# A gated hybrid encoder layer: background weight work in tiles of its own and partly behind the projections, and merge sums that stay on chip

## The chip, the cores and the metric

The kernel runs on one core of one Trainium2 chip. The metric is the device time of one execution in microseconds (us), lower is better. It is given as the median of several runs. A profile comes from one execution of its own. The engines are named as the profile names them: PE multiplies matrices (PEld is its weight load), DVE does elementwise work on vectors, ACT does copies, casts and activations, POOL and SP mainly issue transfers here.

## The reference

One layer of an encoder over 1024 tokens of width 1024, all in float32:

```
h = x + 1/2 * SwiGLU_1(RMSNorm(x))                       # FFN 1, inner width 2816
u = RMSNorm(h)
[qA|kA|vA|qB|kB|vB|gA|gB] = u @ W_in                     # one input projection, width 4352
yA = NeighbourhoodAttention2D(qA, kA, vA)                # 8 heads of 64, 8x16 window, bias table
yB = WindowedGQA(rope(qB), rope(kB), vB)                 # 8 query heads, 2 key heads, window 128, sink
h = h + (sigmoid(gA) * (yA @ W_A) + sigmoid(gB) * (yB @ W_B)) @ W_out      # the merge
h = h + 1/2 * SwiGLU_2(RMSNorm(h))                       # FFN 2, same size as FFN 1
y = RMSNorm_final(h)
SwiGLU(x) = (silu(x @ w_gate) * (x @ w_up)) @ w_down
```

## The kernel before, in words

**Numbers as pairs.** Every operand of a matmul is held as two parts of reduced float32, high and low. `split` writes them: ACT casts the high part, DVE subtracts it from the source to get the low part. One product is then three matmuls in `mm3` (high x high in line 149, high x low in 151, low x high in 153). A program line of a helper therefore stands for many places.

**Strassen products.** The large products are done in 2 x 2 blocks with seven block products, P1 to P7. In the FFNs and the projections, a "product" in the code is one of these for one slice of 128 columns: twelve matmuls 512 wide. `products` runs through them in a fixed order `seq`, prepares the weights of about eight products ahead (`prep_until`), multiplies, and after each product drains its results from PSUM and calls `at_end(n)`, where n counts the products that are still to come (FFN 1 has 154 products, n runs down to 0; the projections have 98).

**Stages in order.** FFN 1 (its first 30 products in an order written out by hand), its down projection (class `Down`), the input projections, the attention with the gates and the branch B product as filler, the branch A products, the merge with W_out (`Down` again, with the name `down`, later `merge`), FFN 2 and its down projection, the final norm.

**Background of FFN 1.** While FFN 1 multiplies, the kernel prepares weights that later stages read back ready split. `later(n, f, ...)` books a step, `behind_ffn1(n)` runs the steps booked for n. There are three sets:

- W_B and the gate columns of W_in that the projections leave out: 8 + 12 = 20 pieces. `wab_fetch` loads a piece into a tile tagged `hs` (six buffers of 128 x 512), `wab_split` writes its two parts into two more `hs` tiles, `wab_put` stores both with a transfer each from POOL's queue. The fetch is booked at n = 108 - 2i, the split two products later, the put one later.
- W_A: `wa_fetch`, `wa_split`, `wa_put`, sixteen splits. These use `split_out`, whose output tile comes from `halves_out`: two buffers tagged `xs`, and as every third one the tile tagged `gain`.
- W_out: `wo_fetch`, `wo_split`, `wo_put`. For each of four row blocks p there are seven splits, 28 in all, with block sums of the weight formed in place in the fetched `hs` tiles; `put_out` stores 512 KB a time into `wo_d`. They are booked from n = 44 down to n = 6.

The splits of these sets are held in program order on their engine by `pin`. Other instructions are ordered by a planner that works with costs when the program is built; it also hands the buffers of a tag to the next tile as they come free. The queue of an engine is then fixed: an instruction that waits holds up what stands behind it on the same engine. `hook(n, f, ...)` books steps behind the projections in the same way.

**Branch A and the gates.** For a row block p, `a_product(p, k)` makes product P1 to P7 in PSUM, `a_keep` lets ACT copy P1, P5 and P6 out, and `a_gate(p, k)` does the rest on DVE: line 1414 adds PSUM to the kept part, line 1416 multiplies by (1 + tanh of the gate) into the gate's own tile `ra`, and for k = P4 and P3, line 1418 adds the whole finished chunk `r` (128 x 1024) to `merged(dc)`, where branch B's part already stands. The gate chunks are fetched by `a_fetch(p)` into tiles tagged `raw` (four buffers, line 1468), and `a_open` applies the tanh on ACT (line 1473). So the buffer of one chunk is free for the fetch of a later one when line 1418 has read it. Branch A runs for p = 0, 1 and then for p = 2, 3, with `both`, `weights`, `a_gate` in the order of the diff's last part.

**Merge.** `Down` multiplies `merged` by the four row blocks of W_out: 7 products x 4 row blocks = 28 entries of twelve matmuls, in the order P2, P1, P5, P6, P3, P7, P4. An entry needs its left operand split (`prep`, lines 95 and 98) and its right operand from `wo_d` (line 591). P1, P2 and P4 take quarters of `merged`. The left operands of P5, P6, P3 and P7 are sums of quarters: `combine(p)` forms four of them on DVE (line 1691) and stores them to `left_d` in DRAM (line 1692); `load_left` brings them back into `raw` tiles (line 577). `combine(0)` and `combine(1)` stand between the branch A products P1/P5 and P2 of p = 2, 3, and `combine(2)` and `combine(3)` behind the first two prepared entries. `evict` (line 639) adds results from PSUM to the residual.

Of the kernel before, what the change touches and what calls it, by code (L numbers as in the profile page):

```python
# [31 lines left out]
def f32v(ap):  # L32
    return ap.bitcast(F32)
# [3 lines left out]
def trunk_kernel(ctx, tc, x, xt, n1, wg1, wu1, wd1, nm, win, rpb, sink, wa, wb, wout,  # L37
                 n2, wg2, wu2, wd2, nf, c_rope, c_mask_a, c_mask_b, out):
    nc = tc.nc
# [9 lines left out]
    ps = ctx.enter_context(tc.tile_pool(name="ps", bufs=4, space=bass.MemoryType.PSUM))  # L49
    dram = ctx.enter_context(tc.tile_pool(name="dram", bufs=1, space=bass.MemoryType.DRAM))  # L50
# [3 lines left out]
    def nm_(s):  # L54
        uid[0] += 1
        return f"{s}_{uid[0]}"
# [8 lines left out]
    ar = {}  # L65
# [26 lines left out]
    pin = tc.keep_in_program_order  # L92
# [15 lines left out]
    def w_cols(w, c0, n=P):  # L108
        return w[:, c0:c0 + n].rearrange("(c p) f -> p c f", p=P)
# [51 lines left out]
    def res(t):  # L161

        return fx[t] if t < 4 else fa[:, (t - 4) * 1024:(t - 3) * 1024]
# [538 lines left out]
    down = down_ffn(wd1[0], lambda t: x2[t])  # L702
# [46 lines left out]
    NG = len(groups)  # L749
    gates = [dc for dc in [*range(8, 16), *range(8)] if 18 + dc not in sum((p for g in groups for p in g), ())]  # L750
    wg_d = dram.tile([len(gates), 2, P, 1024], F32, name="wg_d")
    cast = {}

    def hs(dt):
        return main.tile([P, 512], dt, tag="hs", bufs=6, name=nm_("hs"))

    def wab_fetch(i):
        r = cast[i] = hs(F32)
# [5 lines left out]
        nc.sync.dma_start(r.rearrange("p (c f) -> p c f", f=P), src)  # L764

    def wab_split(i):
        r, h, l = cast[i], hs(F32R), hs(F32R)
        pin(nc.scalar.copy(h, r))
        pin(nc.vector.tensor_tensor(l, r, f32v(h), op=ALU.subtract))
        cast[i] = h, l  # L770

    def wab_put(i):
        g, half = divmod(i - NC8, 2)
        for k, a in enumerate(cast.pop(i)):
            dst = wb_d[i, :, k * 512:k * 512 + 512] if g < 0 else wg_d[g, k, :, half * 512:half * 512 + 512]
            nc.gpsimd.dma_start(dst, f32v(a))

    wo_d = dram.tile([len(PRODUCTS), 4, P, 1024], F32, name="wo_d")
    nout = [0]
    wo = {}  # L780

    def halves_out():

        nout[0] += 1
        if nout[0] % 3 == 0:
            return const.tile([P, 1152], F32R, tag="gain", bufs=1, name=nm_("made"))[:, :1024]
        return main.tile([P, 1024], F32R, tag="xs", bufs=2, name=nm_("made"))

    def split_out(key, src):

        n = src.shape[1]
        o = cast[key] = halves_out()[:, :2 * n]
        pin(nc.scalar.copy(o[:, :n], src))
        pin(nc.vector.tensor_tensor(o[:, n:], src, f32v(o[:, :n]), op=ALU.subtract))

    def put_out(key, dst):
        nc.gpsimd.dma_start(dst, f32v(cast.pop(key)))
# [17 lines left out]
    def later(n, *f):  # L815
        background.setdefault(int(n), []).append(f)
# [22 lines left out]
        put_out((g, p), wa_d[p, g, :, :512] if g == 3 else wa_d[p, g])  # L839

    for i in range(NC8 + 2 * len(gates)):
        for e, f in ((3, wab_put), (2, wab_split), (0, wab_fetch)):
            later(108 - 2 * i - e, f, i)
    for p in range(4):
        later(67 - 5 * p, wa_fetch, p)
        for g in range(4):
            later(64 - 5 * p - 5 * g // 4, wa_split, g, p)
            later(63 - 5 * p - 5 * g // 4, wa_put, g, p)
    step = [44 - 1.34 * k for k in range(29)]
    for p in range(4):  # L850
        later(step[7 * p] + 2, wo_fetch, p)
        for j, k in enumerate(("P2", "P1", "P3", "P5", "P7", "P6", "P4")):
            later(step[7 * p + j], wo_split, k, p)
            later(step[7 * p + j] - 1, wo_put, k, p)

    def behind_ffn1(n):
        down.at_end(n)
# [376 lines left out]
    def hook(n, *f):  # L1234
        hooks.setdefault(n, []).append(f)

    for c in range(5):
        n = 14 * (NG - 1) - 8 - 6 * c
        hook(n, rope_load, c)
        for step in range(3):  # L1240
            hook(n - 4 - step, rope, step, c)
# [166 lines left out]
    def a_gate(p, k):  # L1408

        key, add, dc, n = dict(P2=("X", "P1", p, L), P7=("W", "P5", p + 4, R), P4=("W", None, p + 4, L), P3=("Y", "P6", p, R))[k]  # L1410
        src, r = bk[key, p], mix["ra", dc]
        if add is not None:
            t = kept_a[p, add]
            nc.vector.tensor_tensor(t, src, t, op=ALU.add)
            src = t
        nc.vector.scalar_tensor_tensor(out=r[:, n], in0=r[:, n], scalar=1.0, in1=src, op0=ALU.add, op1=ALU.mult)
        if k in ("P4", "P3"):
            nc.vector.tensor_tensor(merged(dc), merged(dc), r, op=ALU.add)

    def merged(dc):  # L1420
        return slot((0, 1, 2, 3, 24, 25, 26, 27)[dc])
# [248 lines left out]
    def load_h(t):  # L1670
        nc.sync.dma_start(res(t), h_d[t * P:(t + 1) * P, :])


    left_d = dram.tile([4, 4, P, 512], F32, name="left_d")

    def quarter(k, p):
        m = merged(p + (4 if k in ("P2", "P4") else 0))
        return m[:, :512] if k in ("P1", "P2") else m[:, 512:]

    loads = {t: [lambda d, t=t: load_h(t)] for t in range(NTT)}  # L1680
    loads[0].append(lambda d: d.load_left(2))
    down = Down(4, None, 0.5, {}, quarter, {k: left_d[i] for i, k in enumerate(("P5", "P6", "P3", "P7"))},
                loads, (8, 10), late=True, right=wo_d)

    def combine(p):
        a11, a12, a22 = [quarter(k, p) for k in ("P1", "P2", "P4")]
        a21 = merged(p)[:, 512:]
        s = [res(4 + 2 * (p % 2) + k // 2)[:, k % 2 * 512:k % 2 * 512 + 512] for k in range(4)]
        for i, (a, b, op) in enumerate(((a21, a22, ALU.add), (s[0], a11, ALU.subtract), (a12, s[1], ALU.subtract),
                                        (a11, a21, ALU.subtract))):  # L1690
            nc.vector.tensor_tensor(s[i], a, b, op=op)
            nc.gpsimd.dma_start(left_d[i, p], s[i])

    def both(p, *ks):
        for k in ks:
            for q in (p, p + 1):
                a_product(q, k)
                if k in ("P1", "P5", "P6"):
                    a_keep(q, k)
# [7 lines left out]
    for p in (0, 2):  # L1707
        if p:
            both(p, "P1", "P5")
            a_open(3)  # L1710
            combine(0)
            both(p, "P2")
            combine(1)
        both(p, "P6")
        if p == 0:
            a_open(1)
            weights(2, 0)
        for q in (p, p + 1):
            a_gate(q, "P2")
        both(p, "P3")  # L1720
        if p == 0:
            weights(2, 1)
        both(p, "P7")
        if p == 0:
            weights(2, 2)
        for q in (p, p + 1):
            a_gate(q, "P3")
            a_gate(q, "P7")
        both(p, "P4")
        if p == 0:  # L1730
            weights(2, 3)
        for q in (p, p + 1):
            a_gate(q, "P4")
            if p == 0:
                a_fetch(q + 2)
        if p == 0:
            a_open(2)
            for t in range(4):
                new_fx(t)
            new_ar(2)  # L1740
    down.prep_until(2)
    for p in (2, 3):
        combine(p)


# [2 lines left out]
    down = down_ffn(wd2[0], lambda t: h_d[t * P:(t + 1) * P, :])  # L1748
# [22 lines left out]
    late = {}  # L1771
# [111 lines left out]
```

## Time and profile before

| | |
|---|---|
| median of 3 runs | 1930.12 us (1927.0 to 1930.21) |
| profiled execution: its time, its span | 1927.95 us, 1926.2 us |
| PE, PEld busy | 1905.3 us (99%), 1594.1 us (83%) |
| DVE, ACT, POOL busy | 1474.7 us (77%), 961.4 us (50%), 323.6 us (17%) |
| TensorE clock granted, mean | 0.998 |
| DMA | 374.24 MB, mean 194 GB/s |

The span runs from the first to the last instruction, and all times within it are counted from its start. A busy share is the part of the span in which an engine had at least one instruction running. Matmuls overlap on PE, so a matmul's duration is longer than the distance between two starts. A view by windows gives the busy time of each engine within a stretch. A timeline gives start and duration of instructions, with the idle time before them and what ended it in brackets; "x2" there are two merged into one row. "DMA to landing" is the time from the issue of a transfer to its completion.

### The profile page before, as it was taken

The numbers are of one execution on the slowest core, as the hardware profiler recorded it, in microseconds if no ns is written. First come the engines' busy times: TensorE is split into PE (matmuls) and PEld (weight loads), VectorE is DVE, ScalarE is ACT, GpSimd is POOL, SyncE is SP. The second block draws the span as 40 slices with busy tenths as digits, with TensorE's granted clock in tenths as the row PEclk, the third lists the DMA queues.
The fourth block names the chain that finished last, engine by engine and source line by source line (L and its number), as shares of the span: only waits on it lengthen the run. The fifth ranks groups of instructions, "written<-read, shape, count | busy, mean of one in ns | idle before, by whom it ended". The sixth has DMA issues, their size and how long they took to land.

```text
span 1926.2 us, 26199 instructions
## 1 busy us (share of the span) xinstructions
PE 1905.3 (99%) x9020; PEld 1594.1 (83%) x9020; DVE 1474.7 (77%) x2598; ACT 961.4 (50%) x1876; POOL 323.6 (17%) x505
## 2 busy tenths in 40 slices
PE   9999999999999999999999999999999999999998
PEld 7888788888788888898898887788888888888886
DVE  8988878868977778755887999689675566569864
ACT  7533444544346543444888985265333333344453
POOL 0013322213600112211111200010110001005211
PEclk9999999999999999999999999999999999999999
DMA  7258777799353368753647968963422323492341
GB/s 268 94 183 275 260 257 273 296 347 364 96 194 132 111 189 244 232 175 126 178 124 221 280 210 317 371 245 120 148 104 103 121 88 109 145 363 88 119 139 60
DMA packets 184325, 374.24 MB, mean 194 GB/s; under 512 B 18432, under 2 KB 80768, under 8 KB 184192
## 3 DMA queue, kind: packets, MB, share of 16 engines
q1 hardware_dynamic: 146064, 253.01, 39.6%
q0 software_dynamic: 37264, 118.51, 17.9%
q8 instruction: 71, 1.16, 0.2%
q10 hardware_dynamic: 864, 1.05, 0.2%
q14 instruction: 62, 0.51, 0.1%
HBM read 248.25 MB, written 126.02 MB: 194 GB/s over the span
## 4 chain that ended last, share of the span: by engine, by line
PE 85%; DVE 5%; issue 4%; DMA 4%; POOL 1%; ACT 0%; SPq 0%; POOLq 0%; DVEq 0%; ACTq 0%
PE g L149 16%; PE g L151 16%; PE g L153 16%; PE d L153 10%; PE d L151 10%; PE d L149 10%; PE d L1597 2%; DVE ws L98 1%; PE g L1616 1%; PE d L1576 1%; PE d L1577 1%; PE g L1611 1%; DVE ar L98 1%; DMA ar<-in_ffn_w_down_dram 1%; DMA raw<-hid 1%
## 5 line engine op out<-in xcount | busy, mean ns | idle before, releaser
L149 PE MATMUL g<-ar,ws 128*128 128x512 f32 x1072 | 410.3, 394 | 3.5 <-ACT fx L477 1.5
L151 PE MATMUL g<-ar,ws 128*128 128x512 f32 x1072 | 407.4, 390 | 0.0
L153 PE MATMUL g<-ar,ws 128*128 128x512 f32 x1072 | 406.0, 390 | 0.0
L151 PE MATMUL d<-ar,ws 128*128 128x512 f32 x712 | 277.3, 389 | 0.6 <-DVE ar L994 0.6
L149 PE MATMUL d<-ar,ws 128*128 128x512 f32 x712 | 277.6, 390 | 0.2 <-ACT ar L992 0.2
L153 PE MATMUL d<-ar,ws 128*128 128x512 f32 x712 | 277.2, 389 | 0.0
L153 PEld LDWEIGHTS g<-ar,ws 128*128 128x128 f32 x1072 | 201.1, 188 | 41.9
L151 PEld LDWEIGHTS g<-ar,ws 128*128 128x128 f32 x1072 | 201.0, 188 | 41.1 <-DVE ar L98 0.3
L149 PEld LDWEIGHTS g<-ar,ws 128*128 128x128 f32 x1072 | 198.2, 188 | 41.9 <-issue 2.6
L332 DVE TENSOR_TENSOR ws<-raw,ws 128x512 fp32r<-128x512 f32 x216 | 147.6, 688 | 80.5 <-ACT ws L325 79.9
L325 ACT CAST ws<-raw 128x512 fp32r<-128x512 f32 x216 | 132.6, 620 | 132.4 <-PE g L153 62.5
L151 PEld LDWEIGHTS d<-ar,ws 128*128 128x128 f32 x712 | 133.7, 188 | 28.9 <-DVE ar L994 1.2
L149 PEld LDWEIGHTS d<-ar,ws 128*128 128x128 f32 x712 | 133.6, 188 | 28.3 <-ACT ar L992 0.8
L153 PEld LDWEIGHTS d<-ar,ws 128*128 128x128 f32 x712 | 133.7, 188 | 27.9 <-DVE ws L332 0.4
L95 ACT CAST ws<-raw 128x512 fp32r<-128x512 f32 x98 | 61.1, 623 | 139.6 <-PE d L153 57.9
L444 POOL DMA_DIRECT2D hid<-fx x91 | 49.4, 543 | 330.1 <-DVE fx L504 209.2
L98 DVE TENSOR_TENSOR ws<-raw,ws 128x512 fp32r<-128x512 f32 x98 | 73.5, 752 | 39.4 <-ACT ws L95 39.4
L95 ACT CAST ar<-raw 128x512 fp32r<-128x512 f32 (+1 forms) x86 | 55.9, 653 | 94.2 <-PE g L151 52.9
L98 DVE TENSOR_TENSOR ws<-ar,ws 128x512 fp32r<-128x512 f32 x94 | 79.5, 848 | 16.1 <-ACT ws L95 16.0
L149 PE MATMUL g<-ws,ws 128*128 128x512 f32 x232 | 90.9, 392 | 0.0
L153 PE MATMUL g<-ws,ws 128*128 128x512 f32 x232 | 90.4, 390 | 0.0
L151 PE MATMUL g<-ws,ws 128*128 128x512 f32 x232 | 90.3, 389 | 0.0
(360 smaller groups left out, 3916.5 us busy)
## 6 DMA issues: line engine op xcount, KB each, us to landing
raw<-hid SPq DMA_DIRECT2D x70, 512.0 KB
hid<-fx POOLq DMA_DIRECT2D x91, 256.0 KB, 2.7
ar<-in_ffn_w_down_dram SPq DMA_DIRECT2D x32, 512.0 KB
raw<-in_ffn_w_up_dram SPq DMA_DIRECT2D x31, 512.0 KB
wo_d<-made POOLq DMA_DIRECT2D x28, 512.0 KB, 5.8
raw<-in_ffn_w_gate_dram SPq DMA_DIRECT2D x27, 512.0 KB
hid<-fa POOLq DMA_DIRECT2D x51, 256.0 KB, 2.7
ar<-zs_d POOLq DMA_DIRECT2D x48, 256.0 KB, 7.7
```

What stands on the lines that cost most here:

```text
L95: hi = nc.scalar.copy(dst_hi, src)
L98: (eng or nc.vector).tensor_tensor(dst_lo, src, f32v(dst_hi), op=ALU.subtract)
L149: nc.tensor.matmul(b, lhs[0], r[0], start=first, stop=False, **kw)
L151: nc.tensor.matmul(b, lhs[0], r[1], start=False, stop=False, **kw)
L153: nc.tensor.matmul(b, lhs[1], r[0], start=False, stop=last, **kw)
L325: nc.scalar.copy(w[0][:, :512], a)
L332: nc.vector.tensor_tensor(w[0][:, 512:], a, f32v(w[0][:, :512]), op=ALU.subtract)
L444: nc.gpsimd.dma_start(hid[PRODUCTS.index(p), i], src)
L1576: nc.tensor.matmul(b[:, :nw], un["q"][s], un["kd"][s][:, k0 * P:k1 * P], start=True, stop=False)
L1577: nc.tensor.matmul(b[:, :nw], un["q"][s], un["kl"][s][:, k0 * P:k1 * P], start=False, stop=True)
L1597: nc.tensor.transpose(pt[:, i * P:(i + 1) * P], un["pr"][s][:, i * P:(i + 1) * P], ident)
L1611: nc.tensor.matmul(o[:, s], un["v"][s][:, un["k0"] + i, :], un["p"][s][:, i], start=i == 0, stop=i == last)
```

## The change

It does four things.

1. The pieces of W_B and of the gates use `split_out` and `halves_out` for their split parts, so that `hs` holds only their raw form, and both parts go out with one transfer instead of two. The bookings become n = 95 - 1.6i for the split, five products earlier for the fetch, one later for the put. W_A is booked over n = 66 to 38.
2. W_out's row blocks 0 and 1 are booked behind FFN 1 from n = 36 at a step of 1.5 products, and row blocks 2 and 3 behind the projections from n = 27 at a step of 1.34. There `halves_out` gives only the two `xs` buffers (`kept_gain` is emptied).
3. `combine` no longer writes `left_d`. Its sums stay in two tile groups, `ar[1]` and `ar[4]`, taken anew as float32, and `prep` splits them from there. All four calls come after the first six entries of the merge are prepared.
4. Line 1418's addition stays on DVE only for P4 with p = 2 and 3. The other six chunks are added by a transfer from POOL's queue that accumulates `r` onto `merged(dc)`.

```
+    def wab_split(i):
+        split_out(i, wab_raw.pop(i))
...
+            put_out(i, wg_d[g].rearrange("k p f -> p k f")[:, :, half * 512:half * 512 + 512], 2)
...
     for i in range(NC8 + 2 * len(gates)):
-        for e, f in ((3, wab_put), (2, wab_split), (0, wab_fetch)):
-            later(108 - 2 * i - e, f, i)
+        n = int(95 - 1.6 * i)
+        for e, f in ((1, wab_put), (0, wab_split), (-5, wab_fetch)):
+            later(n - e, f, i)
     for p in range(4):
-        later(67 - 5 * p, wa_fetch, p)
...
+        later(66 - 6 * p, wa_fetch, p)
+        for g, e in enumerate((0, 1, 3, 4)):
+            later(61 - 6 * p - e, wa_split, g, p)
+            later(60 - 6 * p - e, wa_put, g, p)
+
+    def wo_steps(put, first, step, ps):
+        for m, p in enumerate(ps):
+            for j, k in enumerate(("P2", "P1", "P3", "P5", "P7", "P6", "P4")):
+                n = int(first - step * (7 * m + j))
+                if j == 0:
+                    put(n + 5 - m, wo_fetch, p)
+                put(n, wo_split, k, p)
+                put(n - 1, wo_put, k, p)
+
+    wo_steps(later, 36, 1.5, (0, 1))
...
+    kept_gain.clear()
+    wo_steps(hook, 27, 1.34, (2, 3))
...
-        if k in ("P4", "P3"):
+        if k == "P4" and p >= 2:
             nc.vector.tensor_tensor(merged(dc), merged(dc), r, op=ALU.add)
+        elif k in ("P4", "P3"):
+            nc.gpsimd.dma_start(merged(dc), r, accum_op=ALU.add)
...
+    COMBINED = ("P5", "P6", "P3", "P7")
     def quarter(k, p):
+        if k in COMBINED:
+            i = COMBINED.index(k)
+            return ar[(1, 4)[i // 2]][:, 2 * (i % 2) + p // 2, p % 2 * 512:p % 2 * 512 + 512]
...
-    loads[0].append(lambda d: d.load_left(2))
-    down = Down(4, None, 0.5, {}, quarter, {k: left_d[i] for i, k in enumerate(("P5", "P6", "P3", "P7"))},
-                loads, (8, 10), late=True, right=wo_d)
+    down = Down(4, None, 0.5, {}, quarter, {}, loads, (8, 10), late=True, right=wo_d)
...
-        s = [res(4 + 2 * (p % 2) + k // 2)[:, k % 2 * 512:k % 2 * 512 + 512] for k in range(4)]
+        s = [quarter(k, p) for k in COMBINED]
...
             nc.vector.tensor_tensor(s[i], a, b, op=op)
-            nc.gpsimd.dma_start(left_d[i, p], s[i])
...
             both(p, "P1", "P5")
             a_open(3)
-            combine(0)
             both(p, "P2")
-            combine(1)
         both(p, "P6")
...
-    down.prep_until(2)
-    for p in (2, 3):
+    down.prep_until(6)
+    for g in (1, 4):
+        new_ar(g, F32)
+    for p in range(4):
         combine(p)
```

More of the change, by code (lines that the diff above doesn't have):

```diff
@@ L751, in trunk_kernel @@
     wg_d = dram.tile([len(gates), 2, P, 1024], F32, name="wg_d")
-    cast = {}
+    cast, wab_raw = {}, {}
     def hs(dt):
@@ L757, in wab_fetch @@
     def wab_fetch(i):
-        r = cast[i] = hs(F32)
+        r = wab_raw[i] = hs(F32)
         if i >= NC8:
@@ L764, in wab_fetch @@
         nc.sync.dma_start(r.rearrange("p (c f) -> p c f", f=P), src)
[L766 to L776, printed above, removed]
     wo_d = dram.tile([len(PRODUCTS), 4, P, 1024], F32, name="wo_d")
-    nout = [0]
+    nout, kept_gain = [0], [True]
     wo = {}
@@ L784, in halves_out @@
         nout[0] += 1
-        if nout[0] % 3 == 0:
+        if nout[0] % 3 == 0 and kept_gain:
             return const.tile([P, 1152], F32R, tag="gain", bufs=1, name=nm_("made"))[:, :1024]
@@ L794, in split_out, with put_out, wab_put @@
         pin(nc.vector.tensor_tensor(o[:, n:], src, f32v(o[:, :n]), op=ALU.subtract))
-    def put_out(key, dst):
-        nc.gpsimd.dma_start(dst, f32v(cast.pop(key)))
+    def put_out(key, dst, parts=1):
+        src = f32v(cast.pop(key))
+        nc.gpsimd.dma_start(dst, src if parts == 1 else src.rearrange("p (k f) -> p k f", k=parts))
+    def wab_split(i):
+        split_out(i, wab_raw.pop(i))
+    def wab_put(i):
+        g, half = divmod(i - NC8, 2)
+        if g < 0:
+            put_out(i, wb_d[i])
+        else:
+            put_out(i, wg_d[g].rearrange("k p f -> p k f")[:, :, half * 512:half * 512 + 512], 2)
     def wo_fetch(p):
@@ L841, in trunk_kernel @@
     for i in range(NC8 + 2 * len(gates)):
-        for e, f in ((3, wab_put), (2, wab_split), (0, wab_fetch)):
-            later(108 - 2 * i - e, f, i)
+        n = int(95 - 1.6 * i)
+        for e, f in ((1, wab_put), (0, wab_split), (-5, wab_fetch)):
+            later(n - e, f, i)
     for p in range(4):
-        later(67 - 5 * p, wa_fetch, p)
[L846 to L854, printed above, removed]
+        later(66 - 6 * p, wa_fetch, p)
[11 more added lines that the diff above has]
+    wo_steps(later, 36, 1.5, (0, 1))
     def behind_ffn1(n):
@@ L1671, in load_h @@
         nc.sync.dma_start(res(t), h_d[t * P:(t + 1) * P, :])
-    left_d = dram.tile([4, 4, P, 512], F32, name="left_d")
+    COMBINED = ("P5", "P6", "P3", "P7")
     def quarter(k, p):
+        if k in COMBINED:
+            i = COMBINED.index(k)
+            return ar[(1, 4)[i // 2]][:, 2 * (i % 2) + p // 2, p % 2 * 512:p % 2 * 512 + 512]
         m = merged(p + (4 if k in ("P2", "P4") else 0))
```

## The prediction

> **What bounds the kernel now.** I read the page's busy table first, then the windows, then what PE waited for, and only then the timeline at the two largest waits.
>
> ```profile
> span 1926.2 us, 26199 instructions
> PE 1905.3 (99%) x9020; PEld 1594.1 (83%) x9020; DVE 1474.7 (77%) x2598; ACT 961.4 (50%) x1876; POOL 323.6 (17%) x505
> ```
>
> PE is the bound, and the change takes no matmul away. What it can win is idle time of PE, 20.9 us in all, part of it before the first and after the last matmul. The windows show where the rest lies (columns: window, length, busy us and count of PE, PEld, DVE, ACT, POOL, then clock, DMA share, GB/s).
>
> ```profile
> 220.00:300.00 80.00, 78.48 (x346) 64.66 (x346) 60.48 (x103) 37.86 (x69) 20.57 (x38) 1.00 0.77 265
> 300.00:420.00 120.00, 120.00 (x531) 99.34 (x531) 98.19 (x161) 60.32 (x108) 28.54 (x53) 1.00 0.82 301
> 500.00:560.00 60.00, 57.41 (x251) 46.56 (x250) 54.84 (x79) 23.82 (x42) 14.91 (x8) 1.00 0.46 146
> 840.00:905.00 65.00, 65.00 (x319) 55.17 (x318) 34.65 (x54) 26.30 (x46) 7.56 (x14) 1.00 0.39 138
> 1165.00:1215.00 50.00, 44.85 (x190) 35.50 (x189) 48.65 (x78) 21.37 (x33) 8.67 (x16) 0.97 0.95 351
> 1215.00:1300.00 85.00, 85.00 (x401) 70.70 (x400) 58.19 (x87) 38.98 (x70) 7.77 (x16) 1.00 0.82 301
> ```
>
> Branch A with the start of the merge (1165 to 1215) loses 5.15 us of PE, at a DVE that is 97% busy and a DMA share of 0.95. FFN 1 loses 1.52 us in 220 to 300. The 2.59 us in 500 to 560 lie in FFN 1's down projection, which the change leaves as it is. The list of PE's waits gives the same places:
>
> ```profile
> PE d L153 <- DVE ws L98: 3.7, 1, 3.7
> PE d L151 <- DVE ws L98: 1.9, 2, 1.6
> PE g L149 <- ACT fx L477: 1.5, 1, 1.5
> PE g L149 <- ACT ar L95: 1.5, 2, 1.3
> ```
>
> **Term 1, FFN 1.** The timeline of the 1.5 us wait:
>
> ```profile
> 217.47 0.38 SPq L764 DMA_DIRECT2D hs<-in_w_in_dram  x1
> 223.97 0.62 ACT L768 CAST hs<-hs 128x512 fp32r<-128x512 f32 x1 [4.66 <-DMA hs<-in_w_in_dram]
> 224.49 0.58 ACT L477 COPY fx<-g 128x512 f32<-128x512 f32 x1
> 225.12 0.50 PE L149 MATMUL g<-ar,ws 128*128 128x512 f32 x1 [1.52 <-ACT fx L477]
> ```
>
> A background cast stands at the head of ACT's queue, and its piece has not landed 6.5 us after the latest fetch before it. Behind it waits the copy that frees a PSUM bank (L477), and PE waits for that. The fetch is booked two products before its split, and a product lasts twelve matmuls at 0.227 us (the starts 1194.65 and 1194.88 below), 2.72 us, so the lead is 5.4 us. The change makes it five products, 13.6 us, and frees the `hs` buffers for raw pieces alone, so SP isn't held up for one. I take the whole 1.52 us as gained; the ends are 0 (another cast waits) and 1.52. The number of casts, subtractions and fetches stays. POOL has 20 issues less, off the path. If the planner puts a fetch later than booked, the same wait comes back.
>
> **Term 2, the start of the merge.**
>
> ```profile
> 1194.65 0.39 PE L151 MATMUL d<-ar,ws 128*128 128x512 f32 x1
> 1194.88 0.39 PE L153 MATMUL d<-ar,ws 128*128 128x512 f32 x1
> ...
> 1202.16 0.39 PE L151 MATMUL d<-ws,ws 128*128 128x512 f32 x1
> 1206.22 1.61 PE L153 MATMUL d<-ws,ws 128*128 128x512 f32 x4 [3.68 <-DVE ws L98]
> ...
> 1210.20 0.41 PE L149 MATMUL d<-ws,ws 128*128 128x512 f32 x1
> ```
>
> ```profile
> 1178.86 1.22 DVE L1418 TENSOR_TENSOR ar<-ar,raw 128x1024 f32<-128x1024 f32 x1
> 1179.99 0.69 DVE L1416 SCALAR_TENSOR_TENSOR raw<-raw,xs 128x512 f32<-128x512 f32 x1
> ...
> 1183.53 1.28 DVE L1416 SCALAR_TENSOR_TENSOR raw<-raw,g 128x512 f32<-128x512 f32 x2
> ...
> 1186.99 0.69 DVE L1691 TENSOR_TENSOR fa<-ar,ar 128x512 f32<-128x512 f32 x1
> ...
> 1191.21 0.69 DVE L1691 TENSOR_TENSOR fa<-ar,fa 128x512 f32<-128x512 f32 x1
> 1191.81 1.28 DVE L1414 TENSOR_TENSOR xs<-g,xs 128x512 f32<-128x512 f32 x2
> ...
> 1194.34 0.69 DVE L1416 SCALAR_TENSOR_TENSOR raw<-raw,xs 128x512 f32<-128x512 f32 x1 [0.65 <-ACT raw L1473]
> ...
> 1203.22 2.35 DVE L1418 TENSOR_TENSOR ar<-ar,raw 128x1024 f32<-128x1024 f32 x2
> 1205.49 1.28 DVE L98 TENSOR_TENSOR ws<-ar,ws 128x512 fp32r<-128x512 f32 x2
> ```
>
> PE has finished branch A at about 1202.2 and lacks the low part of the merge's first left operand. DVE writes it at 1205.49, after a queue without a gap. In that queue stand eight operations of `combine` (1186.99 to 1191.81, 4.82 us) and eight additions of line 1418 at 1.13 us from start to start (1178.86 to 1179.99), 9.0 us. The change takes the first wholly and six of the eight others (6.8 us) out of DVE's way: 11.6 us against a wait of 3.8 us (1206.22 less 1202.16, less one distance). DVE is then no longer late by itself.
>
> The wait has a second price. From 1206.22 to 1210.20 ten matmuls start (the four of the merged row, six single ones), where 0.227 us each make 2.27 us: 1.71 us lost, and the clock column has 0.97 for this window. PE ran at half clock after the gap; after the gaps of 1.5 and 1.6 us listed above the windows show 1.00. So term 2 can give 3.83 + 1.71 = 5.54 us, and a shorter gap than 3.68 us may cost no clock.
>
> The Trainium skill (TensorE: Matmul & The Clock Gate, Part 1: The HAM clock gate) states that about 3.4 us of idling halve the clock and that it stays so for a window of that length. The trace agrees on both sides of it; by that rule a remaining gap under 3.4 us would keep the 1.71 us as gain.
>
> **Term 3, what the accumulating transfers make late.** Line 1418 freed a `raw` buffer at its end; now the buffer is held until a transfer has landed. For p = 2 and 3 the gates are fetched into these buffers, and their tanh was already just in time: DVE waited 0.65 us for it at 1194.34.
>
> ```profile
> 1184.38 3.08 SPq L1468 DMA_DIRECT2D raw<-g_d  x4
> 1193.25 1.06 ACT L1473 ACTIVATE raw<-raw 128x1024 f32<-128x1024 f32 x1 [0.31 <-DMA raw<-g_d]
> ```
>
> No row shows an accumulating transfer. The nearest are plain stores from POOL's queue, of 512 KB each (the first two) and of 256 KB in this very stage (the third):
>
> ```profile
> v_d<-v POOLq DMA_DIRECT2D x4, 512.0 KB, 3.5
> wo_d<-made POOLq DMA_DIRECT2D x28, 512.0 KB, 5.8
> DMA to landing us min/median/max: 3.5/7.0/12.6
> ```
>
> The low end is 3.5 us, the high end twice 12.6 for the doubled size, 25 us. I take 8 us: nearest is the 512 KB store among other traffic (5.8), and reading the destination adds a third pass over the data to two, half as much again, 8.7, a little less because `left_d`'s 16 stores leave this stage.
>
> Follow the chunk whose buffer the third gate fetch takes. Its last product (1183.53) would come at about 1183 with DVE less loaded. Add 8 us, then from fetch to tanh 7.3 us (the third of four issues that begin between 1184.38 and 1187.46 leaves at about 1186, its tanh starts at 1193.25), then 1.06 us: 1199.4, against 1194.3 before. In general it is late by the landing time less 2.9 us. Behind that tanh, DVE's queue holds line 1416 and the additions of P3 and P7, at 0.60 us each (1186.99 to 1191.21 is seven steps), and P4 on PE needs P7's addition. Five such steps put PE's next work at 1202.4, where it is out of branch A work at 1199.2 to 1199.4. That is 3 us, of which the merge's first entries, already prepared by an idle DVE, fill about half (PE takes six of their matmuls early today, 1.4 us). I take 1.5 us of idling as left; the ends are 0 (landing in 3.5 us) and, at 25 us, 20 us late less 5.4 us for two entries, 15 us.
>
> By the Trainium skill (DMA: Bandwidth & Descriptors, Anatomy of one DMA) a store from POOL takes 2.0 us plus its bytes at 436 GB/s; an estimate from that page is 3.2 us for 512 KB, it would make term 3 nothing, and the rows above are longer in every busy stage.
>
> `combine` at its new place costs nothing if it stays hidden. P5 is the first to need a sum, eight entries after 1202.4, so 21.8 us later. DVE has in that time 16 operations (9.6 us), two additions (2.3 us), two products (1.2 us), at most six low parts (3.6 us) and four evictions (2.4 us): 19.1 us. If the cover fails, P5 waits for the part beyond, some 3 us. The 16 stores and 8 loads of `left_d`, 8 MB, leave this stage and the next; six accumulations of 512 KB (three passes, 9 MB against 16 MB) come.
>
> **Term 4, W_out behind the projections.** Fourteen splits move past the projections' queues: on ACT 14 casts, on DVE 14 subtractions and 8 block sums, on SP 8 loads of 256 KB, on POOL 14 stores of 512 KB.
>
> ```profile
> L793 ACT CAST made<-hs 128x512 fp32r<-128x512 f32 (+1 forms) x44 | 26.2, 599 | 16.5 <-DVE hs L807 4.4 <-DMA wa_d<-made 4.4 <-issue 3.0
> L794 DVE TENSOR_TENSOR made<-hs,made 128x512 fp32r<-128x512 f32 (+1 forms) x44 | 29.0, 664 | 19.3 <-ACT made L793 18.6
> ```
>
> That is 14 x 0.62 = 8.7 us on ACT and 22 x 0.69 = 15.2 us on DVE (the full-size forms; the means 599 and 664 ns mix in smaller ones). In 840 to 905, about the products n = 27 to 8, DVE becomes 50 of 65 us, ACT 35, DMA 138 + 9.4 MB in 65 us, 283 GB/s. The window 300 to 420 carries more of each (DVE 98 of 120, 301 GB/s, share 0.82) and PE has 120.00 of 120.00. So the load is hidden. The risk is a wait: with two `xs` buffers a cast may wait for a store (cast 0.62, subtraction 0.69, store 0.53 + 3.5 to 5.8 us make 5.3 to 7.6 us a buffer, 2.7 to 3.8 us a split, and splits come every 3.64 us), and behind it on ACT stand casts and copies that PE needs, as in term 1. I take 0.5 us; ends 0 and 3 us (two waits like that of term 1). The same load gone from 300 to 420 wins nothing, since PE never idled there.
>
> **The sum.** -1.5 (term 1) - 5.5 (term 2) + 1.5 (term 3) + 0.5 (term 4) = -5.0 us, on the profiled execution's 1927.95 us: 1923.0. The median of the runs, 1930.12, stands 2.2 us above that execution, so the predicted median is 1925.1, rounded to 1925.
>
> **The rivals**, each against the median.
>
> 1. Only FFN 1's wait goes, and the late gates give branch A a wait as long as the old one: at a landing time of 12 to 16 us, the 5.5 us are back in full, 1930.1 - 1.5 = about 1929. For it: the DMA share of 0.95, and 7.0 us for 256 KB. Against: the stores that made those 7.0 us came eight at a time, and they go.
> 2. Slower: the accumulating transfer takes 20 us or more. It decides the sign from the point where its wait passes 5.5 + 1.5 us, at a landing of about 16 us; at 25 us it is 15 us plus 1.7 us of clock, less 7, so 1940; at 20 us, 10 + 1.7 - 7, 1935. For it: a read, a second read and a write beside a saturated queue. Against: it needs nearly three times the time of any 512 KB row.
> 3. The change doesn't do what it says behind the matmuls: pinned casts wait again, in FFN 1 or in the projections, for 1.5 us once or twice. Then term 1 is void and term 4 is 3: 1930.1 - 5.5 + 1.5 + 3 = 1929.
> 4. Better: the transfers land in 3.5 us, term 3 is nothing and term 4 too: 1930.1 - 7.0 = 1923. With the form casts before 1168 (1.3 us of wait) also early, 1921.
>
> **How the numbers follow.** Forecast 0.42 (1923 to 1927), rival 1 0.18, rival 2 0.14, rival 3 0.10, rival 4 0.16. A measurement of this kernel tells about 0.2% from no change, 3.9 us. Faster by more: nearly all of the forecast's share and rival 4, 0.56. Within: rivals 1 and 3 with the forecast's edge, 0.28. Slower: rival 2 and a rest, 0.16. The range leaves out the far part of rival 2 and a rest below 1920: 1920 to 1934.
>
> **What would show it.** Term 1: the window 220 to 300 with PE fully busy, and no wait for L477. Term 2: the window around 1165 to 1215 with DVE well under 97%, clock 1.00, no wait of PE for L98 of 3 us. Term 3: landing of `ar<-raw` near 8 us, the wait of ACT L1473 for `raw<-g_d` longer than today's, a PE gap under 2 us. Term 4: 840 to 905 with PE at 65.00. I am wrong if an accumulation lands later than 16 us, or if PE waits in the projections.

## The result: 0.33% slower, and the profile after

| kernel | median | range of its runs | against the kernel before |
|---|---|---|---|
| before, beside it | 1928.64 us | 1925.41 to 1930.47 | 1 |
| changed | 1934.36 us | 1933.35 to 1936.28 | 1.0033 (95% interval 1.0021 to 1.0044) |

The forecast was 1925; the change costs about 6 us. The page and the windows of the changed kernel's profile (columns as before; its program lines from 1400 on have moved by 7 to 10):

```profile
PE 1907.1 (99%) x9020; PEld 1596.2 (83%) x9020; DVE 1468.9 (76%) x2592; ACT 962.5 (50%) x1876; POOL 305.7 (16%) x475
```

```profile
220.00:300.00 80.00, 80.00 (x355) 66.28 (x354) 61.01 (x102) 38.16 (x69) 19.01 (x32) 1.00 0.75 260
500.00:560.00 60.00, 59.87 (x263) 48.93 (x263) 53.19 (x80) 25.14 (x44) 11.80 (x6) 1.00 0.48 157
840.00:905.00 65.00, 64.59 (x291) 53.12 (x289) 43.96 (x72) 32.34 (x58) 13.96 (x26) 1.00 0.75 270
1165.00:1215.00 50.00, 41.11 (x171) 32.30 (x170) 30.01 (x50) 17.80 (x27) 5.25 (x6) 0.93 0.95 285
1215.00:1300.00 85.00, 80.97 (x371) 66.83 (x370) 58.61 (x89) 33.49 (x60) 7.40 (x14) 0.98 0.66 232
```

FFN 1 got better in both its places (80.00 instead of 78.48, 59.87 instead of 57.41). The start of the merge got much worse: 8.9 us of PE idle in 1165 to 1215 where it was 5.15, another 4.0 in the next window, and clocks of 0.93 and 0.98. DVE is no longer the cause, at 30 of 50 us. What PE waits for now:

```profile
PE g L149 <- ACT hs L1413: 6.3, 1, 6.3
PE d L149 <- DMA ws<-wo_d: 4.0, 1, 4.0
PE g L149 <- DMA ws<-wa_d: 1.8, 1, 1.8
PE g L149 <- ACT fa L1115: 1.2, 2, 0.9
```

The accumulating transfers (line 1427, its issues and their way to landing) and what SP, which issues the loads, stood still for between 1180 and 1216 us:

```profile
L1427 POOL DMA_DIRECT2D ar<-raw x6: 857/862/937, 1175.0 to 1206.0; - x6
DMA to landing us min/median/max: 9.4/11.8/15.7
```

```profile
SPq L1477 <- DMA ar<-raw: 15.4, 4, 6.4
SPq L295 <- DMA ar<-raw: 9.6, 2, 9.2
```

Both groups of SP's waits are for the same thing: a `raw` buffer that an accumulation still reads. Line 1477 fetches the gates of the second pair, line 295 a weight of FFN 2. The timeline shows what each does to PE:

```profile
1185.58 10.69 SPq L1477 DMA_DIRECT2D raw<-g_d  x4
1196.84 1.06 ACT L1482 ACTIVATE raw<-raw 128x1024 f32<-128x1024 f32 x1 [13.09 <-DMA raw<-g_d]
1199.06 0.57 ACT L1413 COPY hs<-g 128x512 f32<-128x512 f32 x1
1199.68 0.80 PE L149 MATMUL g<-ar,ws 128*128 128x512 f32 x1 [6.32 <-ACT hs L1413]
...
1213.25 0.33 SPq L295 DMA_DIRECT2D raw<-in_ffn_w_gate_dram  x1
1213.68 1.44 SPq L591 DMA_DIRECT2D ws<-wo_d  x3
1220.21 0.67 PE L149 MATMUL d<-ws,ws 128*128 128x512 f32 x1 [4.03 <-DMA ws<-wo_d]
```

The four gate fetches take 10.69 us to issue instead of 3.08. ACT stands 13.09 us at the first tanh, and the copy that empties P6's bank (line 1413) is queued behind it: PE waits 6.32 us. Then SP stands 9.2 us before the FFN 2 weight of line 295, with W_out's halves of line 591 queued behind: PE waits 4.03 us.

### The profile page after: what moved, and what is told of

Same layout as the page of the kernel before. It is cut to its first block, busy times and chain, and to the rows that moved or that the text cites. A ratio compares the mean times of both kernels' runs of the same rounds, so it can differ in the third digit from the quotient of the medians.

```text
span 1933.4 us, 26137 instructions
## 1 busy us (share of the span) xinstructions
PE 1907.1 (99%) x9020; PEld 1596.2 (83%) x9020; DVE 1468.9 (76%) x2592; ACT 962.5 (50%) x1876; POOL 305.7 (16%) x475
## 4 chain that ended last, share of the span: by engine, by line
PE 91%; DVE 4%; DMA 3%; ACT 1%; issue 1%; SPq 0%; POOLq 0%; POOL 0%; DVEq 0%; ACTq 0%
PE g L149 17%; PE g L151 17%; PE g L153 17%; PE d L151 11%; PE d L153 11%; PE d L149 11%; PE d L1606 2%; DVE ar L98 1%; DVE ws L98 1%; DMA ar<-raw 1%; PE g L1625 1%; PE d L1585 1%; PE d L1586 1%; PE g L1620 1%; PE d L142 1%
## 5 line engine op out<-in xcount | busy, mean ns | idle before, releaser
L332 DVE TENSOR_TENSOR ws<-raw,ws 128x512 fp32r<-128x512 f32 x216 | 147.7, 689 | 81.8 <-ACT ws L325 81.2
L325 ACT CAST ws<-raw 128x512 fp32r<-128x512 f32 x216 | 132.7, 620 | 138.3 <-PE g L153 59.3
L95 ACT CAST ws<-raw 128x512 fp32r<-128x512 f32 x88 | 54.8, 623 | 117.1 <-PE d L153 54.9
L98 DVE TENSOR_TENSOR ws<-ar,ws 128x512 fp32r<-128x512 f32 x104 | 87.7, 844 | 24.2 <-ACT ws L95 24.2
L98 DVE TENSOR_TENSOR ws<-raw,ws 128x512 fp32r<-128x512 f32 x88 | 65.3, 742 | 45.1 <-ACT ws L95 45.0
L149 PE MATMUL g<-ws,ws 128*128 128x512 f32 x232 | 91.0, 392 | 0.0
L95 ACT CAST ws<-ar 128x512 fp32r<-128x512 f32 x104 | 64.2, 618 | 52.9 <-PE g L153 25.1
L153 PE MATMUL g<-ws,ws 128*128 128x512 f32 x232 | 90.5, 390 | 0.0
```

The lines of the kernel that those rows point to most:

```text
L95: hi = nc.scalar.copy(dst_hi, src)
L98: (eng or nc.vector).tensor_tensor(dst_lo, src, f32v(dst_hi), op=ALU.subtract)
L149: nc.tensor.matmul(b, lhs[0], r[0], start=first, stop=False, **kw)
L153: nc.tensor.matmul(b, lhs[1], r[0], start=False, stop=last, **kw)
L325: nc.scalar.copy(w[0][:, :512], a)
L332: nc.vector.tensor_tensor(w[0][:, 512:], a, f32v(w[0][:, :512]), op=ALU.subtract)
```

## The experiments

My theory was that the accumulating transfers alone make the loss, and that the other three parts together gain as forecast. In the table, "us" is the ratio's distance from 1 times 1929; differences between kernels are taken from this column, since their times were measured beside different runs of the kernel before.

| kernel | median | ratio (95%) | us |
|---|---|---|---|
| changed | 1934.36 | 1.0033 (1.0021 to 1.0044) | +6.4 |
| e1 sums on DVE | 1918.34 | 0.9947 (0.9935 to 0.9960) | -10.2 |
| e2 accumulating transfers alone | 1942.78 | 1.0074 (1.0061 to 1.0088) | +14.3 |
| e3 gates in tiles of their own | 1929.13 | 1.0003 (0.9994 to 1.0012) | +0.6 |
| e4 background part alone | 1922.35 | 0.9968 (0.9956 to 0.9981) | -6.2 |
| e6 plain copies in place | 1924.78 | 0.9977 (0.9968 to 0.9986) | -4.4 |
| e7 accumulations of p = 0, 1 | 1928.45 | 0.9999 (0.9990 to 1.0008) | -0.2 |
| e8 accumulations of p = 2, 3 | 1924.43 | 0.9978 (0.9967 to 0.9988) | -4.2 |
| e9 all W_out behind FFN 1 | 1936.73 | 1.0042 (1.0030 to 1.0055) | +8.1 |
| e10 tiles of W_B and gates alone | 1926.06 | 0.9989 (0.9980 to 0.9998) | -2.1 |
| e11 W_out's half nine steps earlier | 1925.15 | 0.9977 (0.9968 to 0.9986) | -4.4 |
| e12 three quarters of W_out moved | 1929.13 | 1.0000 (0.9989 to 1.0012) | 0.0 |

**e1, the changed kernel with every merge sum on DVE.**

```
-        if k == "P4" and p >= 2:
+        if k in ("P4", "P3"):
             nc.vector.tensor_tensor(merged(dc), merged(dc), r, op=ALU.add)
-        elif k in ("P4", "P3"):
-            nc.gpsimd.dma_start(merged(dc), r, accum_op=ALU.add)
```

> The changed kernel with line 1418's sums back on DVE for all eight chunks; everything else of the change stays. Theory (the accumulating transfers hold the gates' buffers for 9 to 16 us, and the late gates hold up ACT, SP and so PE): the waits of PE for ACT L1413 (6.3 us) and for wo_d (4.0 us) go, the merge stage loses at most 3 us of PE, and the gains of FFN 1 and its down projection stay: 4 to 8 us faster than before, ratio 0.996 to 0.998. Rival (the new order of combine and of the six prepared entries is what costs): the merge stage still idles 8 us or more, ratio 1.000 or above.

1918.34 us, the fastest version of this study: 10.2 us faster than before, where 4 to 8 were expected. The sign of the whole change hangs on these six transfers: they cost 10.2 + 6.4 = 16.6 us. The windows of e1:

```profile
1100.00:1165.00 65.00, 63.44 (x367) 55.24 (x366) 59.81 (x174) 52.22 (x132) 0.00 (x0) 0.97 0.76 233
1165.00:1215.00 50.00, 49.07 (x214) 39.52 (x215) 45.08 (x71) 21.75 (x33) 0.00 (x0) 1.00 0.90 329
```

The merge's start has 49.07 us of PE at full clock, with DVE at 45 of 50. So the rival reason for these transfers, that DVE has no time for the sums, doesn't hold once `combine` comes later.

**e2, the kernel before with the accumulating transfers alone** (the diff of e1, applied the other way).

> The kernel before with the accumulating transfers alone (six of the eight sums). Theory: the gates for p = 2 and 3 come some 10 us later, PE waits behind them as in the changed kernel; 6 to 14 us slower than before, ratio 1.003 to 1.007. Rival (order of combine): within 2 us of before.

14.3 us slower, just above the 6 to 14 expected, with the same two waits in the list of e2:

```profile
PE g L149 <- ACT hs L1406: 4.9, 1, 4.9
PE d L149 <- DMA ws<-wo_d: 2.8, 2, 1.5
```

**e3, the second pair's gates in tiles that no accumulation holds.**

```
-            mix["ra", dc] = raw4()
+            mix["ra", dc] = raw4() if p < 2 else res(4 + 2 * (p - 2) + dc // 4)
```

> The changed kernel, accumulating transfers kept, but the gate chunks of p = 2 and 3 are fetched into rows of fa that are free by then, so that no fetch waits for an accumulation to land. Theory (it is the held buffer): tanh of the gates comes before 1192, the waits for ACT L1413 and wo_d go, 4 to 8 us faster than before, ratio 0.996 to 0.998. Rival (the accumulating transfers slow the other loads of a stage whose DMA is 0.95 busy, held buffer or not): PE still waits for wa_d and wo_d, 4 us or more in the stage, ratio 0.999 to 1.002.

That brings back 5.8 of the 16.6 us, and the time is the rival's. The wait behind P6's copy is gone, as the theory said, but the one for W_out's halves stays:

```profile
PE d L149 <- DMA ws<-wo_d: 3.5, 1, 3.5
```

e3 doesn't free every buffer. Its new tiles are now held by the last two accumulations, and SP stands 7.3 us before a load of line 1680 into one of them, with loads of W_out's halves queued behind. So the 5.8 us are not the price of all held buffers. The timeline of e3 also shows a cost without a held buffer: the merge's left operands are split from the accumulated chunks, so ACT's casts wait for the landing itself, and DVE and PE behind them.

```profile
1192.77 0.69 DVE L98 TENSOR_TENSOR ws<-ar,ws 128x512 fp32r<-128x512 f32 x1 [5.27 <-ACT ws L95]
1195.93 0.62 ACT L95 CAST ws<-ar 128x512 fp32r<-128x512 f32 x1 [3.19 <-DMA ar<-raw]
1197.92 0.50 PE L149 MATMUL g<-ar,ws 128*128 128x512 f32 x1 [2.52 <-DVE xs L1421]
```

**e5, both kinds of transfer in a quiet stage.** In the kernel before, POOL moves 512 KB between two idle SBUF tiles during FFN 2, by turns plain and accumulating. In the kernel before, the DMA share from 1305 to 1380 us is 0.40.

```
+        if n <= 92 and n >= 50 and n % 6 == 2:
+            nc.gpsimd.dma_start(trial["b"], trial["a"])
+        if n <= 92 and n >= 50 and n % 6 == 5:
+            nc.gpsimd.dma_start(trial["b"], trial["a"], accum_op=ALU.add)
```

> The kernel before, with 512 KB transfers from one SBUF tile to another issued by POOL in the quiet part of FFN 2, alternately plain and accumulating, on tiles that nothing else uses then; the sums are of zeros and used by nobody. Theory (the accumulation itself makes a transfer slow): the plain ones land in 3 to 4 us and the accumulating ones in 6 us or more. Rival (it is only the load of the merge stage that made 11.8 us): both kinds land within 1 us of each other, at 3 to 5 us. The time of the kernel is expected within 2 us of the kernel before.

The two lines in the trace of e5, plain first:

```profile
L1759 POOL DMA_DIRECT2D xs<-trial_a x8: 532/543/552, 1309.8 to 1378.4; - x8
...
DMA to landing us min/median/max: 2.8/3.4/6.0
```

```profile
L1761 POOL DMA_DIRECT2D xs<-trial_a x7: 861/881/926, 1312.9 to 1373.2; - x7
...
DMA to landing us min/median/max: 4.5/4.9/6.4
```

Between the two expectations: the accumulation adds 1.5 us to a quiet landing, and 0.34 us to POOL's issue (0.88 against 0.54). Neither explains 11.8 us; the stage does the rest. The kernel took 1931.8 us in its one run, 2.5 us above the median of the kernel before beside it (1929.31), whose own runs reach 1932.09.

**e6, six plain copies in the places of the accumulations** (the sums of the merge are left out).

```
-            nc.gpsimd.dma_start(merged(dc), r, accum_op=ALU.add)
+            nc.gpsimd.dma_start(merged(dc), r)
```

> The changed kernel with its six accumulating transfers turned into plain copies of the same 512 KB between the same tiles (so the sums of the merge are left out and the merged chunks hold one term). Everything else, the order and every wait, is kept. Theory (the accumulation is what is slow): median landing falls from 11.8 us to 4 to 7 us and the time to 1920 to 1925 us, near the 1918.3 of the sums on DVE. Rival (six more transfers in a stage whose DMA engines are full, of whatever kind): landing stays at 9 us or more and the time at 1930 to 1936 us.

A mixed answer. In this stage even a plain copy lands late, so the rival has the landing time; the theory has the time of the kernel, 1924.8:

```profile
DMA to landing us min/median/max: 6.4/9.2/9.8
```

Of the 16.6 us, any 512 KB transfers at these places cost 5.8, and the accumulation the other 10.8. The software queue's share of the DMA engines between 1165 and 1215 us (columns: packets, MB, share of 16 engines) shows a difference, for the kernel before, the changed kernel and e6 in turn:

```profile
q0 software_dynamic: 1167, 3.86, 19.3%
```

```profile
q1 hardware_dynamic: 3336, 11.09, 63.4%
q0 software_dynamic: 860, 3.15, 31.6%
```

```profile
q1 hardware_dynamic: 4235, 14.37, 79.3%
q0 software_dynamic: 864, 3.15, 15.5%
```

For the same 3.15 MB the accumulation takes twice the engine time: 31.6% of 16 engines over 50 us are 253 us, against 124 for plain copies, whose price per MB is that of the stores before (154 us for 3.86 MB). The quiet stage of e5 has the same price, in two windows that hold nothing but one plain transfer (1350.4 to 1353.5 us) and one accumulating (1345.55 to 1350.3 us):

```profile
q0 software_dynamic: 144, 0.52, 42.2%
```

```profile
q0 software_dynamic: 144, 0.52, 58.1%
```

That is 21 us of engine time for the plain one and 44 us for the accumulating one, so the factor of two doesn't come from the load of the stage. In the merge stage it is taken where the engines are full (share 0.95 in both kernels), and the loads on the other queue, among them those for PE, move 11.09 MB instead of 14.37. SP's waits for held buffers may be part of that drop; no run separates the two.

**e7 and e8, accumulations for the first pair only (four) and for the last two only.**

```
-        if k == "P4" and p >= 2:
+        if k in ("P4", "P3") and p >= 2:          # e7
+        if k == "P4" or k == "P3" and p < 2:      # e8
```

> The changed kernel with accumulating transfers only for the four sums of the first pair (P3 and P4 of p = 0 and 1), and DVE sums for p = 2 and 3. Theory (the first four hold the buffers of the gates that the second pair needs and so block ACT's queue, 6.3 us, with 1.8 us at a left-operand load; the last two delay only the load of W_out's halves, 4.0 us): 1926 to 1931 us, 8 to 12 us above the sums on DVE, and the wait for wo_d is under 1 us. Rival (the last two cost most, since they stand nearest to what follows): 1919 to 1923 us.

> The changed kernel with accumulating transfers only for the two sums P3 of p = 2 and 3, the others on DVE. Theory: the wait of PE behind the P6 copy is gone, the load of W_out's halves is late by up to 4 us behind an FFN 2 weight load that waits for a buffer: 1918 to 1923 us. Rival (the last two cost most): 1926 to 1932 us.

Each keeps one of the two waits, in the lists of e7 and of e8:

```profile
PE g L149 <- ACT hs L1413: 7.3, 1, 7.3
```

```profile
PE d L149 <- DMA ws<-wo_d: 3.4, 1, 3.4
```

The window of e8 that holds this second wait keeps its full clock:

```profile
1165.00:1215.00 50.00, 46.44 (x204) 37.18 (x203) 45.37 (x72) 20.37 (x32) 1.81 (x2) 1.00 0.94 326
```

Against e1, four transfers cost 10.0 us and two cost 6.0; together 16.0 of the 16.6. The two waits are separate chains, one through ACT's queue and one through SP's. e7's time is as expected, e8's is 1.4 us above its expected range.

**e4 and e10, the background alone.** e4 is the kernel before with parts 1 and 2 of the change, the merge as before. e10 has only the tiles and bookings of W_B and the gates; W_A and W_out are booked as before, all behind FFN 1.

```
     # e10, kept from the kernel before
+    step = [44 - 1.34 * k for k in range(29)]
+    for p in range(4):
+        later(step[7 * p] + 2, wo_fetch, p)
...
-    wo_steps(later, 36, 1.5, (0, 1))
...
-    wo_steps(hook, 27, 1.34, (2, 3))
```

> The kernel before with the new background of FFN 1 and the half of W_out behind the projections; merge as before. Theory: the window 220 to 300 and 500 to 560 gain 1.5 and 2.5 us as in the changed kernel, the projections' end loses 1 to 2, the merge's 3.7 us wait and its clock loss stay: 1 to 5 us faster, ratio 0.9975 to 0.9995. Rival (the 2.5 us in 500 to 560 came from the merge's tiles, not from this part): only 0 to 1 us faster.

> The kernel before with only the first part of the change: W_B's and the gates' halves in the tiles and by the helper of W_out's halves, from step 95 down; w_A's and all of W_out's steps at their places of before, behind FFN 1, and the merge as before. Theory (FFN 1's wait at 235 us was the tiles', the 2.6 us between 500 and 560 us were W_out's steps crowding FFN 1's tail): 220 to 300 us has its full 80.00 us of PE, 500 to 560 us still 57 to 58, and the time is 1925 to 1928 us. Rival (all of the FFN 1 gain comes from the tiles): 59.8 in 500 to 560 us and 1921 to 1923 us.

e4, windows and its largest wait:

```profile
500.00:560.00 60.00, 59.87 (x263) 48.92 (x262) 53.13 (x80) 25.15 (x44) 11.81 (x6) 1.00 0.49 155
1165.00:1215.00 50.00, 46.22 (x195) 36.76 (x194) 48.29 (x74) 18.86 (x29) 8.64 (x16) 0.97 0.97 351
```

```profile
PE d L153 <- DVE ws L98: 3.6, 1, 3.6
```

e10, windows:

```profile
220.00:300.00 80.00, 80.00 (x355) 66.26 (x354) 63.77 (x110) 40.13 (x73) 21.15 (x36) 1.00 0.82 287
500.00:560.00 60.00, 57.31 (x250) 46.40 (x249) 53.67 (x78) 23.00 (x41) 13.45 (x7) 1.00 0.49 148
```

The tiles give 2.1 us and remove the wait near 225 us. Moving the rest gives another 4.1 us (e4 less e10), and there the window 500 to 560 goes from 57.31 to 59.87. e9 below has the new tiles and W_A's new places but all of W_out behind FFN 1, and PE loses 4.98 us in that window. So that loss came from W_out's steps behind FFN 1. How it reaches so far is only in part clear. In the kernel before, the last subtraction of these steps starts at 414.3 us, and PE waits for DVE's line 98 at 518.92 and 522.91 us (1.62 and 0.96 us). Between the two, from 460 to 480 us, the DMA share is 1.00 there and 0.94 in e10, against 0.38 in e4. A backlog of transfers that makes DVE late is likely, but not shown.

e10's time and windows are as its theory said. e4's gain of 6.2 us is above the 1 to 5 expected. e4 keeps the merge's old wait of 3.6 us and its clock of 0.97; from e4 to e1, part 3 is worth 4.0 us.

**e9, e11 and e12, other places for W_out's steps,** all on e1 (in e9 the line with `hook` is taken out).

```
-    wo_steps(later, 36, 1.5, (0, 1))
-    wo_steps(hook, 27, 1.34, (2, 3))
+    wo_steps(later, 36, 1.2, range(4))          # e9
+    wo_steps(hook, 36, 1.34, (2, 3))            # e11, later(...) as in e1
+    wo_steps(later, 34, 3.0, (0,))              # e12
+    wo_steps(hook, 38, 1.34, (1, 2, 3))         # e12
```

> The version with all merge sums on DVE (1918.3 us) with all of W_out's halves prepared behind FFN 1 (28 steps from step 36 down, 1.2 apart) and none behind the projections. Theory (the half behind the projections costs the 1.2 us that TensorE waits at their tail, and is not needed once W_B and the gates use other tiles): the stretch from 840 to 1100 us gets 1 us shorter, the one from 500 to 560 us stays within 0.5 us, and the time is 1916 to 1918 us. Rival (FFN 1's tail has no room for 28 steps): 500 to 560 us again loses 2 to 3 us and the time is 1919 to 1922 us.

> The version with all merge sums on DVE (1918.3 us) with its half of W_out behind the projections nine steps earlier (from step 36 instead of 27 down). Theory (at the projections' tail W_out's transfers slow the read-back of the rotated channels, whose casts hold TensorE's PSUM copies in ACT's queue): the wait at 905 to 920 us goes and the time is 1916.5 to 1918 us. Rival (the steps now meet the rotations' own transfers around 740 to 760 us, where this version loses 1.0 us already): that loss grows and the time is 1919 to 1922 us.

> The version with all merge sums on DVE with only one quarter of W_out's halves (p = 0, steps 3 apart) behind FFN 1 and three quarters (p = 1, 2, 3, from step 38 down, 1.34 apart) behind the projections. Theory (FFN 1's tail is free of waits with half of W_out already, so nothing is left to gain there, while the projections carry half as much again): 500 to 560 us stays at 59.8 to 60.0 and the time is 1918 to 1922 us. Rival (the projections have room and FFN 1 still loses): 1915 to 1917 us.

None of the three improves on e1, and e9 and e11 lie above what either side expected. e9 is 18.3 us above e1. Its rival named one place of the loss, 500 to 560 us, and there 2 to 3 us where PE loses 4.98 (the window below); 300 to 500 us loses another 7.15.

```profile
500.00:560.00 60.00, 55.02 (x232) 42.58 (x231) 58.83 (x73) 21.84 (x39) 25.29 (x15) 1.00 0.43 138
```

In e11 the loss behind 905 us goes, as its theory said (0.01 us of PE idle in 905 to 1000 us, against 0.80 in e1), but PE now stops for 4.04 us at 872 us. The timelines of e9 and of e11 show one mechanism (line 781 is the background cast that was line 793 before):

```profile
422.74 0.62 ACT L781 CAST made<-hs 128x512 fp32r<-128x512 f32 x1 [4.57 <-DMA wo_d<-made]
423.78 0.58 ACT L477 COPY fx<-g 128x512 f32<-128x512 f32 x1
424.41 0.61 PE L149 MATMUL g<-ar,ws 128*128 128x512 f32 x1 [1.79 <-ACT fx L477]
```

```profile
871.27 0.62 ACT L781 CAST made<-hs 128x512 fp32r<-128x512 f32 x1 [3.70 <-DMA wo_d<-made]
871.79 0.59 ACT L1115 ACTIVATE fa<-g 128x512 f32<-128x512 f32 x1
872.44 0.79 PE L149 MATMUL g<-ar,ws 128*128 128x512 f32 x1 [4.04 <-ACT fa L1115]
```

A background cast has no output buffer, because an earlier store to `wo_d` hasn't landed, and the copy that frees a PSUM bank stands behind it on ACT. In e9 this is the smaller of two such waits. Before the larger, 3.85 us at 418.22 us, ACT stood 5.06 us ahead of a cast of line 781, and the profile doesn't name what ended that.

e12 has PE fully busy in 500 to 560 us, as its theory said, but is 7 us above its range. Its list of PE's waits has the wait of e11 again, where e1 has 0.8 us:

```profile
PE g L149 <- ACT fa L1115: 6.5, 3, 2.7
```

Between 830 and 920 us ACT's casts of line 781 wait 10.2 us for stores to `wo_d`, in e1 0.8 us. So the projections don't hold three quarters of W_out without waits. e12's runs scatter from 1924.8 to 1936.3 and the profiled execution is the fastest of them, so where the rest of its median goes stays open.

## Why the prediction was wrong, point by point

From run to run the parts measure -2.1 us (the tiles, e10), -4.1 (the moved steps, e10 to e4), -4.0 (the sums on chip, e4 to e1) and +16.6 (the accumulating transfers, e1 to the changed kernel). The forecast had -1.5, +0.5, -5.5 and +1.5.

**Term 1 was right.** The window 220 to 300 has 80.00 us of PE, the wait for line 477 is gone, and e10 measures 2.1 us (0.4 to 3.9) where 1.5 were forecast.

**Term 2 was right in mechanism and too large in size.** Without the accumulating transfers (e4 to e1) the wait for line 98 is gone and the clock in 1165 to 1215 is back at 1.00. That is worth 4.0 us between the medians, not 5.5. e1's profiled execution, the slowest of its five runs, has a new clock loss just before (0.97 in 1100 to 1165); whether that is what is missing in the median isn't shown. `combine` is hidden at its new place, as worked out: no wait of PE in e1 names it. In the changed kernel itself none of this can be seen, because term 3 takes the place.

**Term 3 is the step that failed:** 16.6 us where I took 1.5 and gave 15 as the far end.

- The landing time was a small part of the error. I took 8 us; it was 9.4 to 15.7 with a median of 11.8, well inside the ends of 3.5 and 25. In the prediction's working the term grows by one us per us of landing, so 11.8 us would have given about 5.3 us (an estimate), 3.8 of the 15.1 us that were missing.
- "Behind that tanh, DVE's queue holds line 1416" followed the wrong queue. ACT's own queue holds P6's copy behind the tanh, and PE needs that copy at once; and as ACT also makes the casts of the merge's left operands, behind the same tanh (the first starts at 1200.95 us, after PE has gone on at 1199.68), the entries that were to fill the gap weren't ready. So the sign turned well below the 16 us of landing that I named.
- I followed only one user of the held buffers. FFN 2's weight load also wants a `raw` tile, and on SP it stands ahead of W_out's halves; that second chain has 4.0 us of waiting, and with it the last two transfers cost 6.0 us (e8).
- I priced the transfer by its landing and not by the engine time that it takes from others. My three passes against two would have given half as much again; the traces show twice (253 against 124 us of engine time for the six), in a stage with a DMA share of 0.95.

Rival 2 had the sign and nearly the time (1935 at its near end), but not its condition, a landing of 20 us or more. Rival 1 is nearer in landing (12 to 16 us) and expected 1929, since it gave the late gates a wait of only 5.5 us. Neither has ACT's copy or SP's queue in it. "Nearly three times the time of any 512 KB row" held against a landing of 20 us, but the loss didn't need one.

**Term 4 had the wrong sign.** In the projections the size was near: in 840 to 905 PE loses 0.41 us in the changed kernel and 0.52 in e4, with 0.78 and 0.19 more in 905 to 1000, against 0.5 forecast. The loads are near it too (DVE 43.96 against 50, ACT 32.34 against 35, 270 against 283 GB/s). But I wrote that the 2.59 us in 500 to 560 lie in work "which the change leaves as it is", and that the load gone from FFN 1 wins nothing, having looked at 300 to 420 alone. The down projection's code stays as it is, but not its time: W_out's steps were booked down to n = 6, right before it, and the 2.56 us that it regains without half of them are most of the 4.1 us between e10 and e4.

**The range** ended at 1934 and the median is 1934.36: rival 2 had 0.14 and I cut it off where it began.

## What to carry to other kernels

Price a transfer that replaces an elementwise operation by three things: its landing in the stage where it runs, the engine time that it takes there from the loads on the critical path, and every queue that waits for a buffer which it now holds. Walk each of those queues, the one that issues loads included, to the next instruction that the bounding engine needs. When background work is moved, look for its price at the place that it leaves as carefully as at the one that it goes to.

## What the hardware showed that I had not expected

- An accumulating SBUF-to-SBUF transfer of 512 KB lands in 4.9 us in a quiet stage against 3.4 us for a plain one, and in 11.8 against 9.2 us where the DMA share is 0.95. It takes about twice the engine time (44 against 21 us for one alone). The estimate of 3.2 us that the prediction worked out from the Trainium skill (DMA: Bandwidth & Descriptors, Anatomy of one DMA) agrees with the plain quiet transfer alone.
- PE's clock can fall without a long gap. In e1 PE was idle for 1.6 us in all between 1155 and 1165 us (0.63 and 0.69 us in the two longest gaps), and had these clocks:

```profile
1155.00:1160.00 5.00, 3.59 (x16) 2.60 (x15) 4.96 (x12) 2.72 (x7) 0.00 (x0) 0.86 0.81 293
1160.00:1165.00 5.00, 4.85 (x20) 3.71 (x18) 2.99 (x8) 2.58 (x5) 0.00 (x0) 0.80 0.50 175
```

  The Trainium skill (TensorE: Matmul & The Clock Gate, Part 1: The HAM clock gate) names about 3.4 us of idling as the condition. The trace agrees for the single gap of e4 (3.6 us, clock 0.97 in 1165 to 1215 us), and that of e8 is at the edge (3.4 us, clock 1.00). It doesn't agree for e3, where a gap of 2.5 us at 1195 us is followed by clocks of 0.85 and 0.81 (1195 to 1200 and 1200 to 1205 us), nor for these shorter ones of e1; what decides there stays open.
